# Layer 0's opening by pairs of feature tiles: norm, V and the first q and k from modulation quarters

## The chip, the core and the metric

One core of a Trainium2 chip runs the whole program once. The core has five engines with a queue each: TensorE (PE, matmuls into PSUM), VectorE (DVE), ScalarE (ACT), GpSimd (POOL) and SyncE (SP, which here issues nearly all DMAs). The metric is the device time of one execution in microseconds: 965.41 us as the median of 3 runs (965.35 to 966.09). Below, 1 MB is a million bytes, and a load of 1024 KB is 1.05 MB.

## The reference, cut to what matters

The network has 256 tokens of 1024 features, two transformer layers (attention, then a gated feed-forward) and a third layer with a convolution module. All of it is in 32-bit floats. Each norm is modulated by vectors that come from a conditioning vector c. What the change touches is the start of layer 0:

```python
c_act = jax.nn.silu(c)
mod = (c_act @ ada_w[0] + ada_b[0])[:, None, :]          # ada_w[0]: 1024 x 6144
sh_a, sc_a, g_a, sh_f, sc_f, g_f = jnp.split(mod, 6, axis=-1)
h = rms_norm(x, norm_g[0, 0]) * (1.0 + sc_a) + sh_a
q, k, v = jnp.split(h @ w_qkv, 3, axis=-1)               # w_qkv: 1024 x 3072, 8 heads of 128
```

Before the first projection can start, two of the six vectors (the scale sc_a and the shift sh_a) are needed; each is the product of c_act with a 1024 x 1024 block of ada_w[0], 4.19 MB. After that comes attention over 256 tokens with a bias by relative position, the output projection, and the feed-forward with the other four vectors.

## The kernel before, in words

Layout. The normed input is kept turned: `T` holds 8 feature tiles of 128 features (partitions) by 256 tokens. Every matmul operand is kept as a high part (a rounded 32-bit form for TensorE) and a low part (the rest), and `mm3` (L137 to L140) makes each product by three matmuls: high by high, high by low, low by high. A weight load (`load`, SP, L81) brings 1.05 MB into a raw buffer; `split` (L97 to L113) makes the high parts on ScalarE (L109, 1024 columns) and the low parts on VectorE (L111, 512 columns). `rows_unit` loads 256 rows by 1024 columns in runs of 4 KB, `cols_unit` and `half_unit` load 256-column blocks in runs of 1 KB. There are 4 raw buffers, and the first three loads rest in tiles that are not used yet (`spare`). The split parts have 8 buffers for high and 8 for low parts.

The opening. `first_norm` (L296) reads the two vectors' weights one after the other, each in four loads of 1.05 MB (the last in halves), and multiplies them with silu(c) on TensorE (`quads`, L232): the weights are the moving operand, the broadcast column of c the stationary one, four 32-column groups side by side. x is read behind the third load. The summed row gets its bias (L318), for the scale also one added and the gain multiplied (L320), is turned to columns by TensorE (L323, L325), and the normed and turned x (`nb`, L331 to L341) is multiplied by the scale columns on VectorE (L344). `shifted` adds the shift on ScalarE (L352) and makes the low part on VectorE (L353), two feature tiles at a time, ahead of each unit of the V projection.

Then `project` makes V in four units of 256 rows (`rows_matmul`, 512-column matmuls); units are loaded, split and multiplied one after the other. The bias tiles of attention are turned into `nb` by eight matmuls (L387). Pairs of heads follow: for each of four pairs, q and then k by `cols_matmul` (48 matmuls of 256 columns each), and the attention blocks of a pair run among the matmuls of the next pair (`step`). The output projection and the residual close the stage.

Background. The other 16 modulation vectors of the network are made by `mod_sum` (L204 to L218): four loads of 1.05 MB each, two products of 1024 columns per load on VectorE (L214, L216), ordered behind the newest split. `bg_step` is called after each unit and each q or k block, and `bg_plan` gives each stage a number of steps and of slots: in the first stage, 12 steps over 10 slots, the first two calls skipped. Those twelve steps are the three vectors that the end of this stage needs (the gate, the next scale, the next shift). A finished row is stored to DRAM (L226) and read back broadcast (`bcast_coef`, L181).

Order. Each engine works its queue in order. The order is not the text's: the framework's planner puts an instruction ahead of earlier ones that are not ready by its own reckoning (the copies of L448, traced in the first feed-forward, run at 2.5 us).

## Time and profile before

| what | value |
|---|---|
| median of 3 runs | 965.41 us |
| profiled execution, its own time | 965.92 us |
| its span, first to last instruction | 964.1 us |
| mean granted TensorE clock | 0.992 |
| HBM read, mean rate over the span | 240.94 MB, 252 GB/s |

The profiled execution is 0.5 us above the median, and 1.8 us of it lie outside the span. Times in rows are microseconds from the span's start. In a row `out<-in` names the tile written and the tiles read; `th` and `tl` are the high and low part of `T`, `h` and `l` (in the first unit `park`) those of a weight, `raw` a loaded weight. `[2.20 <-ACT park L109]` is the idle time of the engine before the instruction and what ended it. `x4` counts instructions.

### The profile page before, as it was taken

The page shows a single profiled execution, that of the slowest core. Times are in us where ns is not written, and L with a number is a line of the kernel's source. Part 1 is how long each engine was busy: PE and PEld are TensorE (multiplying, and loading weights), DVE is VectorE, ACT ScalarE, POOL GpSimd, SP SyncE. Part 2 cuts the span into 40 slices and gives each one's busy share as a digit, 9 for nine tenths or more (in the row PEclk, how much of TensorE's full clock was granted, in tenths as well). Part 3 has the DMA queues.
Part 4 walks back from the last instruction along what each step waited for, and adds up shares of the span by engine and source line. Part 5 has one row for each costly group of instructions (what it writes and reads, how often), then busy time and mean ns, then how long its engine had stood idle before and what let it go on. Part 6 is the DMA issues. An engine that isn't in the chain of part 4 may idle for free.

```text
span 964.1 us, 17220 instructions
## 1 busy us (share of the span) xinstructions
PE 929.8 (96%) x6687; PEld 812.9 (84%) x6687; DVE 765.9 (79%) x1461; ACT 495.1 (51%) x870; POOL 50.0 (5%) x118
## 2 busy tenths in 40 slices
PE   5899999999999999999999999999998999999997
PEld 2579977998999879876789999988897779999996
DVE  2778978977878798787999878888877789977774
ACT  2345666543344455685643444546416745655552
POOL 2100000000000010122100000001000100000000
PEclk9899999999999999999999999999999999999999
DMA  9988985978879859664589899886846366965511
GB/s 349 401 300 287 335 284 176 323 279 332 271 263 375 305 194 366 228 220 132 175 295 336 284 335 328 290 306 200 285 114 206 128 214 226 303 231 184 175 45 44
DMA packets 141519, 244.06 MB, mean 253 GB/s; under 512 B 6662, under 2 KB 106174, under 8 KB 141438
## 3 DMA queue, kind: packets, MB, share of 16 engines
q1 hardware_dynamic: 140918, 241.64, 72.2%
q0 software_dynamic: 496, 1.31, 0.4%
q8 instruction: 52, 0.85, 0.4%
q14 instruction: 29, 0.24, 0.1%
q10 hardware_dynamic: 24, 0.01, 0.0%
HBM read 240.94 MB, written 2.01 MB: 252 GB/s over the span
## 4 chain that ended last, share of the span: by engine, by line
issue 43%; PE 38%; DVE 7%; DMA 6%; ACT 3%; POOL 3%; SPq 1%; DVEq 0%; POOLq 0%; ACTq 0%
PE up L140 6%; PE up L139 6%; PE up L138 6%; PE acc L138 5%; PE acc L140 5%; PE acc L139 5%; DVE l L111 2%; DMA raw<-in_moba_w_qkv_dram 2%; DMA raw<-in_ada_w_dram 1%; DMA x<-in_x_dram 1%; PE acc L869 1%; ACT junk L485 1%; DMA raw<-in_ffn_w_in_dram 1%; POOL rstd L492 1%; PE up L659 1%
## 5 line engine op out<-in xcount | busy, mean ns | idle before, releaser
L111 DVE TENSOR_TENSOR l<-raw,h 128x512 fp32r<-128x512 f32 x548 | 354.6, 684 | 72.5 <-ACT h L109 70.2
L109 ACT ACTIVATE h<-raw 128x1024 fp32r<-128x1024 f32 x274 | 280.2, 1054 | 163.1 <-PE up L139 40.4
L140 PE MATMUL up<-th,l 128*128 128x256 f32 x640 | 181.6, 284 | 0.0
L139 PE MATMUL up<-tl,h 128*128 128x256 f32 x640 | 181.2, 283 | 0.0
L138 PE MATMUL up<-th,h 128*128 128x256 f32 x640 | 180.8, 283 | 0.0
L216 DVE SCALAR_TENSOR_TENSOR gemv<-raw,c_s,gemv 128x1024 f32<-128x1024 f32 x112 | 143.2, 1278 | 1.2 <-DMA raw<-in_ada_w_dram 0.2
L138 PEld LDWEIGHTS up<-th,h 128*128 128x128 f32 x640 | 121.0, 189 | 2.0 <-DVE m L759 0.4
L140 PEld LDWEIGHTS up<-th,l 128*128 128x128 f32 x640 | 120.7, 189 | 0.1
L139 PEld LDWEIGHTS up<-tl,h 128*128 128x128 f32 x640 | 120.4, 188 | 0.4
L138 PE MATMUL acc<-h,mh 128*128 128x512 f32 x232 | 91.6, 395 | 0.0
L139 PE MATMUL acc<-l,mh 128*128 128x512 f32 x232 | 90.7, 391 | 0.0
L140 PE MATMUL acc<-h,ml 128*128 128x512 f32 x232 | 90.4, 392 | 0.0
L140 PE MATMUL up<-oh,l 128*128 128x256 f32 x288 | 81.9, 284 | 0.0
L139 PE MATMUL up<-ol,h 128*128 128x256 f32 x288 | 81.8, 284 | 0.0
L138 PE MATMUL up<-oh,h 128*128 128x256 f32 x288 | 81.1, 282 | 0.0
L138 PE MATMUL acc<-th,h 128*128 128x256 f32 x256 | 74.9, 293 | 0.4 <-ACT h L109 0.4
L140 PE MATMUL acc<-th,l 128*128 128x256 f32 x256 | 73.3, 286 | 0.2 <-DVE l L111 0.2
L139 PE MATMUL acc<-tl,h 128*128 128x256 f32 x256 | 73.1, 286 | 0.0
L138 PEld LDWEIGHTS up<-oh,h 128*128 128x128 f32 x288 | 54.6, 190 | 0.8
L139 PEld LDWEIGHTS up<-ol,h 128*128 128x128 f32 x288 | 54.2, 188 | 0.7
L140 PEld LDWEIGHTS up<-oh,l 128*128 128x128 f32 x288 | 54.4, 189 | 0.1
L138 PEld LDWEIGHTS acc<-h,mh 128*128 128x128 f32 x232 | 43.6, 188 | 11.0 <-issue 1.6
(230 smaller groups left out, 1667.9 us busy)
## 6 DMA issues: line engine op xcount, KB each, us to landing
raw<-in_ada_w_dram SPq DMA_DIRECT2D x46, 1024.0 KB
raw<-in_ffn_w_in_dram SPq DMA_DIRECT2D x36, 1024.0 KB
raw<-in_mod_w_dram SPq DMA_DIRECT2D x24, 1024.0 KB
raw<-in_ffn_w_out_dram SPq DMA_DIRECT2D x22, 1024.0 KB
raw<-in_f_up_w_dram SPq DMA_DIRECT2D x18, 1024.0 KB
raw<-in_moba_w_qkv_dram SPq DMA_DIRECT2D x12, 1024.0 KB
raw<-in_diff_w_qkv_dram SPq DMA_DIRECT2D x12, 1024.0 KB
raw<-in_f_down_w_dram SPq DMA_DIRECT2D x11, 1024.0 KB
```

What stands on the lines that cost most here:

```text
L109: newest["high"] = nc.scalar.activation(h, r, AF.Copy).ins
L111: newest["split"] = nc.vector.tensor_sub(l[:, k], r[:, k], h[:, k].bitcast(F32)).ins
L138: nc.tensor.matmul(ps, lh, rh, start=start, stop=False, skip_group_check=True)
L139: nc.tensor.matmul(ps, lh, rl, start=False, stop=False, skip_group_check=True)
L140: last = nc.tensor.matmul(ps, ll, rh, start=False, stop=stop, skip_group_check=True).ins
L216: nc.vector.scalar_tensor_tensor(t, src, c[:, k:k + 1], t, op0=ALU.mult, op1=ALU.add)
L485: nc.scalar.activation(junk, src, AF.Square, scale=1.0 / 32, accum_out=ss[:, i:i + 1])
L492: nc.gpsimd.tensor_tensor(r, v, mhalf, op=ALU.pow)
L659: nc.tensor.matmul(po[:, 0:P], *(lr[::-1] if diff else lr), start=i == 0, stop=i == blk)
L869: mm = nc.tensor.matmul(ps[32 * g:32 * g + 32, 0:P], lw[t][:, m, g, :], ur[:, g, 4 * m:4 * m + P], start=m == 0, stop=m == 7, tile_positio ...
```

## The change

The two vectors are no longer read one after the other. `first_load` reads both at once in quarters of 256 columns, as eight DMAs of 0.26 MB (128 partitions, two runs of 1 KB each); the quarters rest in tiles of other uses (quarters 0 and 2 in the three coefficient tiles and the tile of the background sum, quarters 1 and 3 in the two q tiles and one buffer each of the split's high and low parts). `first_rows` reads and norms x first. `first_tiles` makes the scale and shift columns of two feature tiles from a quarter: quarters 0 and 1 by TensorE (8 matmuls of 512 columns, copied by ScalarE), quarters 2 and 3 by VectorE (8 products of 512 columns), then four one-column matmuls per quarter; two small VectorE operations apply bias, one and gain. ScalarE writes the high part straight from `nb` with scale and bias, and once more as a plain float, from which VectorE takes the low part.

`first_project` goes through four pairs of feature tiles: for each tile the V matmuls (four accumulators) and those of q and k of the first pair of heads (two accumulators). So pair 0 is finished with V, and the loop over pairs begins at pair 1. The q and k weights of pair 0 come by `half_unit` (512 rows by 256 columns of each). The bias tiles' loads are traced after the first quarter, their turning into `nb` after V. The silu of the second conditioning vector is ordered behind the norm. The first stage's background plan skips no call; with six calls in the pairs instead of eight and none in V, its twelve steps fall 2, 2, 1, 1, 1, 1 in pairs 1 to 3 and four in the output projection.

```diff
+FIRST_ON_PE = 2
...
-    def split(raw, blocks=False, rooms=None):
+    def split(raw, blocks=False, rooms=None, after=None):
...
-            newest["high"] = nc.scalar.activation(h, r, AF.Copy).ins
+            with tc.issue_after(after) if after else nullcontext():
+                newest["high"] = nc.scalar.activation(h, r, AF.Copy).ins
...
+    def rows_load(w, k0, c0):
+        return load(lambda raw: [(raw.rearrange("p (k n) -> p k n", k=2),
+                                  w[k0 * P:k0 * P + 256, c0:c0 + 1024].rearrange("(k p) n -> p k n", p=P))])
     def rows_unit(w, k0, c0, rooms=None):
-        return split(load(lambda raw: [(
-            raw.rearrange("p (k n) -> p k n", k=2),
-            w[k0 * P:k0 * P + 256, c0:c0 + 1024].rearrange("(k p) n -> p k n", p=P))]), rooms=rooms)
+        return split(rows_load(w, k0, c0), rooms=rooms)
...
+    pick = one.tile([P, 1], F32, name="pick")
+    nc.gpsimd.memset(pick, 0.0)
+    for i in range(4):
+        nc.gpsimd.memset(pick[32 * i:32 * i + 1, :], 1.0)
...
-        nc.scalar.activation(cs, c, AF.Silu)
-        return cs
+        return cs, lambda: nc.scalar.activation(cs, c, AF.Silu)
...
-    def mod_load(w, j, r, halved=False):
+    def mod_load(w, j, r):
...
-    def quads(ps, c, k, src, start, stop):
...
-    def first_norm(T):
...
+    def first_columns():
+        rows = work.tile([24, P], F32, name="rowsm", tag="w")
+        w, b, c = jobs[0][0], jobs[0][1], jobs[0][5]
+        for i, v in enumerate((b[D:2 * D], b[0:D], jobs[0][3])):
+            nc.scalar.dma_start(rows[8 * i:8 * i + 8, :], v.rearrange("(k p) -> k p", p=P))
+        ps = tr.tile([P, 512], F32, name="tr")
+        nc.tensor.transpose(ps[:, 0:24], rows, ident[:24, :24])
+        col = one.tile([P, 3, 8], F32, name="mcol")
+        nc.vector.tensor_copy(col.rearrange("p i k -> p (i k)"), ps[:, 0:24])
+        nc.vector.tensor_scalar(col[:, 0, :], col[:, 0, :], 1.0, None, op0=ALU.add)
+        return col
+    def first_rows():
+        for h in range(2):
+            nc.sync.dma_start(x[:, h, :], a["x"][0, h * P:h * P + P, :])
+        for h in range(2):
+            ss = small.tile([P, 2], F32, name="ss")
+            src = halves(x[:, h, :])
+            for n in range(2):
+                squares(ss, n, src[n])
+            r = rstd_of(ss)
+            for n in range(2):
+                t = two.tile([P, 512], F32, name="hn")
+                nc.vector.tensor_scalar(t, src[n], r, None, op0=ALU.mult)
+                ps = tr.tile([P, 512], F32, name="tr")
+                for q in range(4):
+                    nc.tensor.transpose(ps[:, q * P:q * P + P], t[:, q * P:q * P + P], ident)
+                ins = nc.scalar.activation(nb[:, 4 * n:4 * n + 4, h * P:h * P + P],
+                                           ps.rearrange("p (k n) -> p k n", k=4), AF.Copy).ins
+        return ins
+    def first_load(t):
+        w = jobs[0][0]
+        tiles = []
+        for i in range(4):
+            where, tag = (((coef, "coef"), (coef, "coef"), (coef, "coef"), (one, "gemv")),
+                          ((two, "q"), (two, "q"), (hlp, "h"), (hlp, "l")))[t % 2][i]
+            m = where.tile([P, 2, 2, 256], F32, name="fmod", tag=tag)
+            for n, j in enumerate((1, 0)):
+                nc.sync.dma_start(m[:, n], w[:, j * D + 256 * t:j * D + 256 * t + 256].rearrange(
+                    "(p r) n -> p r n", r=8)[:, 2 * i:2 * i + 2, :])
+            tiles.append(m)
+        return tiles
+    def first_tiles(T, t, rows, col, on_pe):
+        c = jobs[0][5]
+        g = two.tile([P, 2, 256], F32, name="fgem", tag="hn")
+        if on_pe:
+            ps = tr.tile([P, 512], F32, name="tr")
+            for r in range(8):
+                q = 32 * (r % 4)
+                nc.tensor.matmul(ps[q:q + 32, :], c[:, r:r + 1].to_broadcast([P, 32]), rows[r // 2][:, :, r % 2, :],
+                                 start=r < 4, stop=r >= 4, tile_position=(0, q), skip_group_check=True)
+            nc.scalar.activation(g.rearrange("p j n -> p (j n)"), ps, AF.Copy)
+        else:
+            for r in range(8):
+                src = rows[r // 2][:, :, r % 2, :]
+                if r == 0:
+                    nc.vector.tensor_scalar(g, src, c[:, 0:1], None, op0=ALU.mult)
+                else:
+                    nc.vector.scalar_tensor_tensor(g, src, c[:, r:r + 1], g, op0=ALU.mult, op1=ALU.add)
+        ps = tr.tile([P, 512], F32, name="tr")
+        for j in range(2):
+            for b in range(2):
+                nc.tensor.matmul(ps[:, 2 * j + b:2 * j + b + 1], g[:, j, b * P:b * P + P],
+                                 pick if on_pe else ones32[:, 0:1], start=True, stop=True, skip_group_check=True)
+        m = small.tile([P, 4], F32, name="fcols")
+        k = 2 * t
+        nc.vector.tensor_tensor(m, ps[:, 0:4], col[:, 0:2, k:k + 2], op=ALU.add)
+        nc.vector.tensor_tensor(m[:, 0:2], m[:, 0:2], col[:, 2, k:k + 2], op=ALU.mult)
+        for b in range(2):
+            v = work.tile([P, S], F32, name="fv", tag="w")
+            for d in (T[0][:, k + b, :], v):
+                nc.scalar.activation(d, nb[:, k + b, :], AF.Identity, scale=m[:, b:b + 1], bias=m[:, 2 + b:3 + b])
+            nc.vector.tensor_sub(T[1][:, k + b, :], v, T[0][:, k + b, :].bitcast(F32))
+    def first_project(w):
+        T = new_T("t")
+        col = first_columns()
+        turned = first_rows()
+        vals = [[acc.tile([P, 512], F32, name="acc") for _ in range(2)] for _ in range(2)]
+        qk = [up.tile([P, 512], F32, name="up") for _ in range(2)]
+        vw, qw = {}, {}
+        def load_v(u):
+            vw[u] = rows_unit(w, 2 * u, 2 * D)
+        def load_qk(u):
+            qw[u] = half_unit(w, u, (0, D))
+        def values(k):
+            wh, wl = vw[k // 2][k % 2]
+            for h in range(2):
+                for n in range(2):
+                    sl = slice(512 * n, 512 * n + 512)
+                    mm3(vals[h][n], *tok(T, k, h), wh[:, sl], wl[:, sl], k == 0, k == NK - 1)
+        def heads(k):
+            wh, wl = (t[:, k % 2, :] for t in qw[k // 4][k // 2 % 2])
+            for i in range(2):
+                for b in range(2):
+                    sl = slice(256 * i + 128 * b, 256 * i + 128 * b + 128)
+                    mm3(qk[i][:, 256 * b:256 * b + 256], wh[:, sl], wl[:, sl], T[0][:, k, :], T[1][:, k, :],
+                        k == 0 and b == 0, k == NK - 1)
+        def tiles_of(t):
+            first_tiles(T, t, mods.pop(t), col, t < FIRST_ON_PE)
+        mods = {0: first_load(0)}
+        raw = {0: rows_load(w, 0, 2 * D)}
+        mods[1] = first_load(1)
+        tiles_of(0)
+        next(bias)
+        with tc.issue_after(turned):
+            make_c2()
+        vw[0] = split(raw.pop(0), after=turned)
+        load_qk(0)
+        for t in range(NK // 2):
+            if t < 3:
+                load_v(t + 1)
+            if t + 2 < 4:
+                mods[t + 2] = first_load(t + 2)
+            if t == 1:
+                load_qk(1)
+            if t + 1 < 4:
+                tiles_of(t + 1)
+            for k in (2 * t, 2 * t + 1):
+                values(k)
+                heads(k)
+        return T, qk, vals
...
-        for h, ps in project(T, w_qkv, 2 * D, ("oh", "ol"), before=first):
-            for n in range(2):
-                nc.scalar.activation(v[:, h, 512 * n:512 * n + 512], ps[n], AF.Copy)
+        pairs = []
+        scale = -float(DH // (2 if diff else 1)) ** -0.5
+        def pair(pq, pk):
+            q = two.tile([P, 2, S], F32, name="q")
+            nc.scalar.activation(q, pq.rearrange("p (b n) -> p b n", b=2), AF.Copy, scale=scale)
+            yield
+            kk = two.tile([P, 2, S], F32, name="kk")
+            nc.scalar.activation(kk, pk.rearrange("p (b n) -> p b n", b=2), AF.Copy)
+            pairs.append((q, kk))
         if first:
+            T, qk, vals = first_project(w_qkv)
+            for h, ps in enumerate(vals):
+                for n in range(2):
+                    nc.scalar.activation(v[:, h, 512 * n:512 * n + 512], ps[n], AF.Copy)
+            for _ in pair(*qk):
+                pass
             next(bias)
             lam_col()
+        else:
+            for h, ps in project(T, w_qkv, 2 * D, ("oh", "ol")):
+                for n in range(2):
+                    nc.scalar.activation(v[:, h, 512 * n:512 * n + 512], ps[n], AF.Copy)
...
-        for i in range(4):
+        if first:
+            heads(0)
+        for i in range(len(pairs), 4):
...
-    plans = ((12, 10, 2), (16, 17), (12, 12), (20, 17), (0, 0), (4, 4, 4))
+    plans = ((12, 10, 0), (16, 17), (12, 12), (20, 17), (0, 0), (4, 4, 4))
```

## Rows read from the trace of the kernel before

**Rows 1.** Page part 1: busy us, share of span, instructions, by engine.

```profile
PE 929.8 (96%) x6687; PEld 812.9 (84%) x6687; DVE 765.9 (79%) x1461; ACT 495.1 (51%) x870; POOL 50.0 (5%) x118
```

**Rows 2.** Waits of PE in 0 to 32 us: total, times, longest.

```profile
PE acc L232 <- DMA raw<-in_ada_w_dram: 10.8, 6, 7.0
```

**Rows 3.** Chain of waits, 0 to 60 us: start, us, what.

```profile
2.67 11.27 DMA x<-in_x_dram
...
22.32 6.55 DMA raw<-in_ada_w_dram
```

**Rows 4.** Timeline of PE: start, us, engine, line, operation, count, idle before.

```profile
23.25 1.93 PE L232 MATMUL acc<-raw,c_s 128*32 128x256 f32 x32
...
32.75 0.80 PE L138 MATMUL acc<-park,th 128*128 128x512 f32 x1 [2.20 <-ACT park L109]
...
60.15 1.88 PE L387 MATMUL tr<-toep,stage 128*128 128x512 f32 x4
...
74.04 0.28 PE L140 MATMUL acc<-th,l 128*128 128x256 f32 x1
74.16 0.28 PE L138 MATMUL acc<-th,h 128*128 128x256 f32 x1
```

**Rows 5.** Windows: length, busy PE, PEld, DVE, ACT, POOL; clock, DMA share, GB/s.

```profile
0.00:10.00 10.00, 1.94 (x16) 0.69 (x16) 1.43 (x5) 1.70 (x3) 3.81 (x14) 1.00 0.78 266
10.00:20.00 10.00, 6.55 (x49) 2.99 (x50) 1.86 (x4) 4.08 (x10) 1.97 (x4) 0.87 1.03 405
20.00:30.00 10.00, 7.26 (x84) 3.19 (x83) 4.14 (x14) 1.08 (x2) 1.28 (x2) 0.96 1.03 409
```

**Rows 6.** Windows of pair 0's k and pair 1's q.

```profile
66.00:72.00 6.00, 5.39 (x43) 4.99 (x42) 4.12 (x6) 2.49 (x3) 0.00 (x0) 1.00 1.06 379
72.00:78.00 6.00, 6.00 (x53) 6.00 (x52) 5.13 (x9) 2.85 (x4) 0.00 (x0) 1.00 1.05 375
```

**Rows 7.** Page part 5: ScalarE's split, the high part.

```profile
L109 ACT ACTIVATE h<-raw 128x1024 fp32r<-128x1024 f32 x274 | 280.2, 1054 | 163.1 <-PE up L139 40.4
```

**Rows 8.** Windows of the V projection.

```profile
32.70:38.00 5.30, 5.25 (x13) 4.15 (x14) 5.27 (x10) 4.44 (x7) 0.00 (x0) 0.52 1.03 384
38.00:57.50 19.50, 19.50 (x85) 15.55 (x83) 16.48 (x21) 6.62 (x9) 0.00 (x0) 1.00 0.99 377
```

**Rows 9.** Groups of 32 to 80 us: ScalarE's feature rows of layer 0.

```profile
L352 ACT ACTIVATE th<-nb,col 128x256 fp32r<-128x256 f32 x6 | 2.7, 494 | 0.0
```

**Rows 10.** Groups of VectorE, 73.4 to 137.9 us.

```profile
L111 DVE TENSOR_TENSOR l<-raw,h 128x512 fp32r<-128x512 f32 x43 | 28.1, 685 | 2.6 <-ACT h L109 2.5
L216 DVE SCALAR_TENSOR_TENSOR gemv<-raw,c_s,gemv 128x1024 f32<-128x1024 f32 x11 | 14.1, 1278 | 0.0
```

**Rows 11.** Windows of pairs 1 to 3 and the output projection.

```profile
73.40:118.00 44.60, 44.60 (x366) 42.85 (x364) 41.01 (x96) 27.05 (x62) 0.00 (x0) 1.00 0.90 321
118.00:138.00 20.00, 19.39 (x109) 15.32 (x108) 14.87 (x44) 13.72 (x34) 0.00 (x0) 1.00 0.87 276
...
100.00:120.00 20.00, 20.00 (x164) 18.69 (x163) 18.54 (x47) 14.94 (x35) 0.00 (x0) 1.00 0.91 334
```

**Rows 12.** Timeline of SP's queue, 104 to 140 us.

```profile
104.64 10.06 SPq L81 DMA_DIRECT2D raw<-in_moba_w_o_dram  x4
120.29 0.53 SPq L226 DMA_DIRECT2D scratch<-row  x1
120.86 1.39 SPq L181 DMA_DIRECT2D coef<-scratch  x3
122.35 17.93 SPq L81 DMA_DIRECT2D raw<-in_ffn_w_in_dram  x9
```

**Rows 13.** Timeline: VectorE's last output-projection split, TensorE's first feed-forward matmul.

```profile
126.31 1.88 DVE L111 TENSOR_TENSOR l<-raw,h 128x512 fp32r<-128x512 f32 x3
...
148.26 0.39 PE L138 MATMUL up<-park,th 128*128 128x512 f32 x1
```

**Rows 14.** Waits of SP's queue in 0 to 45 us: total, times, longest.

```profile
SPq L81 <- DMA raw<-in_ada_w_dram: 12.7, 5, 3.8
```

89 lines of the change are left out of this document (10 added, 79 removed).

## The prediction

> **What bounds the kernel now.** I read the page's busy times first. TensorE is busy in 96% of the span [rows 1], so a change pays only where TensorE now waits, and it loses wherever it adds TensorE work or a new wait. Next come the waits of TensorE in the first 32 us: 10.8 us go to DMAs of the modulation weights [rows 2]. The chain of waits says what stands there: x lands at 2.67 + 11.27 = 13.94 us, and the last modulation piece ends 6.55 us after 22.32 us [rows 3]. The timeline then shows the first V matmul at 32.75 us, released by ScalarE's split of the first V weights, and the last matmul of pair 0 (q and k) at 74.04; pair 1 starts at 74.16 [rows 4]. The windows show DMA at its rate throughout: 405 and 409 GB/s between 10 and 30 us [rows 5]. So the opening is bound by bytes: two modulation vectors of 4.19 MB each must be in before any projection can start, and after 32.75 us TensorE is bound by its own work. The reader is to see that the opening is the only large hole.
>
> The quantity I work out is the start of pair 1, 74.16 us now. All TensorE work after it is the same in both kernels, so the time moves with it, less what is given back later.
>
> **Bytes up to pair 1.** The new order on SP is x (1.05 MB), modulation quarter 0 (2.10), V rows 0 (1.05), quarter 1, q/k half 0, V rows 1, quarter 2, V rows 2, quarter 3, q/k half 1, V rows 3: 15.7 MB, and 1.05 MB of bias tiles beside them. x and V (5.24 MB) come in 4 KB runs, at 0.405 MB/us [rows 5]: 12.9 us. Quarters, q/k and bias tiles (11.5 MB) come in 1 KB runs. Their rate follows from the stretch where 1 KB column loads and 4 KB modulation loads alternate at 379 and 375 GB/s [rows 6]: 2/0.377 - 1/0.405 gives 0.353 MB/us, so 32.7 us. The first 10 us moved 2.66 MB [rows 5], as if a full-rate stream began at 3.4 us. x landed 1.4 us after its bytes (3.4 + 3.67/0.405 = 12.5, against 13.94 [rows 3]). The last V rows thus land at 3.4 + 12.9 + 32.7 + 1.4 = 50.4 us. One ScalarE split, 1.05 us [rows 7], and the last two feature tiles follow: 24 V matmuls at 19.5/85 = 0.23 us [rows 8] and 24 of 256 columns at 0.12 us [rows 4], 8.4 us. By bytes pair 1 starts at 59.9 us.
>
> A rule bears on this. The modulation loads become 32 DMAs of 0.26 MB in place of DMAs of 0.5 and 1 MB. The Trainium skill (DMA: Bandwidth & Descriptors, section Bandwidth) asks for transfers of 1 MiB or more, and its fit in the section on the anatomy of a DMA (2.0 us plus bytes over 436 GB/s, for the GpSimd path) gives, as an estimate from that page, 2.6 us for each, 83 us for the 32 if they ran one by one. The windows of 10 to 30 us [rows 5] show a queue kept at its rate by several DMAs in flight, which is against reading the rule that way here; no row shows DMAs of this size in a stream.
>
> **TensorE up to pair 1.** x, quarter 0 and V rows 0 land at 3.4 + 5.2 + 5.9 + 1.4 = 15.9 us. ScalarE then makes four feature rows at 0.49 us [rows 9] and one split: the first V matmul comes at 19.0, 13.7 us earlier than now. From there: 96 V matmuls, 22.2 us; 96 of 256 columns, 11.4; the start at half clock, where 13 matmuls took 5.30 us at a granted 0.52, nearly all of it at the 1.2 GHz level, after an engine that had stood 2.2 us [rows 4, 8], in place of 3.0 us, so 2.3; two modulation quarters on TensorE, 16 instructions of 512 columns each, against 32 of 256 in 1.93 us [rows 4], so 1.9 us each; the column picks, four small ones per quarter, bounded by nothing and by 1 us, taken at 0.9, so 3.6; the bias flips, 2 us (four take 1.88 while other matmuls run among them [rows 4]). Sum 19.0 + 22.2 + 11.4 + 2.3 + 3.8 + 3.6 + 2.0 = 64.3 us, if TensorE never waits. If flips and picks fall into waits for data, the bytes decide: 60. If the clock stays at the lower level for the first two quarters, half of the projection work takes twice as long, up to 16.8 us more. I take 64, as the work row is the longer: a gain of 10 us in the start of pair 1.
>
> What is removed costs nothing more: the row path (transposes, row and gain adds, eight scalings, x behind the modulation) stood before 32.75 and goes whole. What is added on other engines hides in a stage paced by bytes: eight more feature rows on ScalarE, 4 us over 45; on VectorE 16 half-length products for quarters 2 and 3, some 0.64 us each by half of 1.28 [rows 10], 10.2 us. From 27 to 52 us VectorE then has those, three units of V and one of q/k (four subtractions each, at 28.1/43 = 0.65 us [rows 10]) and the low parts, about 22 us in 25: covered, but only just. The ACT queue's three small loads change shape, not number; the silu of the second c moves behind the norm and is needed only in layer 2; the bias-tile loads on POOL's queue are in the byte sum.
>
> **What is late next: VectorE in pairs 1 to 3 and the output projection.** The background plan changes from 12 steps over ten slots that all lie before the output projection to 8 in the blocks of pairs 1 to 3 and 4 in that projection. Each step is 1.05 MB and two products of 1.28 us. Between 73.4 and 138 us VectorE is busy 41.0 + 14.9 = 55.9 of 64.6 us, with 11 of these long products and one short one, 14.8 us [rows 10, 11]. All 24 would be 30.7, so 15.9 us come in. Two steps (5.1 us) can be done between the last V rows and pair 1, and six subtractions for the next stage (3.9 us) can slide: 62.8 of 64.6 us. TensorE now stays full with VectorE at 18.54 of 20 us [rows 11], 93%; at that share 60 us fit, so 3 us come out as TensorE waits for split weights. Bounds: nothing, if VectorE's 8.7 us of idle time there close up, and 10.8 us, the 15.9 less the two early steps, if none does. I take 3, by the stretch at 93%.
>
> The last vector of that plan also comes later. Now its store is issued at 120.29, its broadcast loads follow at 120.86, and the feed-forward loads stand behind them in SP's queue at 122.35 [rows 12]; they are first used at 148.26 [rows 13]. Afterwards the twelfth step stands behind the last output-projection split, which ends at 128.2 now [rows 13]; four steps of 2.56 us put it at 138.4 on the old clock. If the feed-forward loads stay behind it (some 2.5 us for store and broadcast, then the 9.9 us that the first one takes now, 122.35 to 132.2, and a split), 5 us show. If SP is given them earlier, as the four output-projection loads at 104.64 stand ahead of the store, nothing shows. I take nothing, by that row.
>
> **Sum.** 10 - 3 = 7 us. The profiled execution took 965.92 us (span 964.1, 1.8 around it), so 958.9; the median of the three runs is 0.5 lower, so 958.4 for the median, written 958.5.
>
> **Rivals.**
> First, nothing is given back: flips and picks fall into waits, pair 1 starts near 61, VectorE's waits close up: 965.4 - 13 = 952. For it: VectorE's idle time in that stretch is mostly waiting. Against: the stage is full on three engines. Chance 0.20.
> Second, VectorE and the hand-over take nearly all: 9 us or 4 + 5 instead of 3, so 964, between 962 and 967. For it: the 62.8 of 64.6 us. Against: SP's order at 104.64. Chance 0.18.
> Third, the stages do not interleave as written, because quarter 3 rests in buffers that splits and the first pair's q also use, and what follows in SP's queue (q/k half 1, V rows 3) waits with it. SP waits for such releases today: 12.7 us behind landed DMAs alone in the first 45 us [rows 14]. If quarter 3 starts 6 us late, pair 1 starts at about 68 to 70 and VectorE gives back 1: 962. Chance 0.12.
> Fourth, slower: the 32 small DMAs do not keep the rate. The 8.39 MB of quarters take 23.8 us at 0.353; below about 0.24 MB/us they take 11 us more, the 7 us gain and the 4 us by which TensorE's sum exceeds the byte sum are gone, and from there the kernel loses. At half the rate it is 24 us more: 965.4 - 7 - 4 + 24 = 978. The rule on transfer size in the Trainium skill (DMA: Bandwidth & Descriptors, section Bandwidth) speaks for this rival. Against it: SP issues three loads in 1.39 us, 0.46 each [rows 12], and the bytes of one small DMA take 0.74 us, so the queue can be kept filled. Chance 0.08.
>
> **How the numbers follow.** The forecast has 0.42, with a range of its own from 955 to 962. A measurement of this kernel tells 0.2%, 1.9 us, from no change. Faster than 963.5: 0.42 + 0.20 + 0.10 + 0.06 = 0.78. Within: 0.10 from the second and third. Slower than 967.3: 0.08 of the fourth and 0.04 of the second, 0.12. The range of 949.5 to 967 leaves out 0.08 above with the fourth, some of the second, and a little below.
>
> **What would show it.** Right: the first V matmul near 19 us; DMA at 350 GB/s or more up to 50; the last V rows landing near 50; pair 1's first matmul at 60 to 66; VectorE over 90% busy from there to the end of the output projection, with new TensorE waits on its subtractions of some 3 us in all. The forecast is wrong if pair 1 starts after 70, if the granted clock stays at 0.5 beyond the first quarter, if the quarters move below 250 GB/s, or if TensorE stands over 5 us at the start of the first feed-forward.

## The result, and the profile after

The changed kernel takes 973.06 us (median of 4 runs, 971.29 to 973.66) against 965.75 us (965.35 to 967.46) beside it: a ratio of 1.0069, interval 1.0054 to 1.0085. It is slower by 0.7%; 958.5 was forecast, and the range ended at 967. Its profiled execution is the quickest of the four: 971.29 us, span 969.5, so the profile holds 5.4 us of span to be found, of 7.3 between the medians; what the slower executions add is not seen in it.

Two instants cut the loss: the start of pair 1 (74.16 before [rows 4]) and the transposes of the second token half's feed-forward norm. TensorE's timeline has them (start, us, engine, line, operation, count, idle before), first of the kernel before, then of the changed one:

```profile
156.52 0.60 PE L527 MATMUL tr<-ident,hn 128*128 128x128 f32 x4
```

```profile
68.95 3.69 PE L465 MATMUL tr<-toep,stage 128*128 128x512 f32 x8
72.08 0.68 PE L142 MATMUL acc<-th,h 128*128 128x256 f32 x1
...
162.55 0.60 PE L605 MATMUL tr<-ident,hn 128*128 128x128 f32 x4
```

The bias flips end at 72.64, and pair 1 is in full course at 72.6: 1.5 us earlier than before, where 10 were forecast. From there to the second half's norm it takes 89.9 us, before 82.4: 7.5 given back, where 3 were forecast. Behind that norm 0.6 us come back (its distance to the end of the span is 807.6 us before, 807.0 after). -1.5 + 7.5 - 0.6 = 5.4.

**The opening.** Windows of the changed kernel, columns as in [rows 5]:

```profile
10.00:20.00 10.00, 6.31 (x40) 4.33 (x38) 2.02 (x7) 5.24 (x11) 1.28 (x3) 0.98 1.08 358
20.00:30.00 10.00, 8.43 (x35) 3.36 (x35) 2.16 (x7) 4.66 (x7) 0.53 (x1) 0.67 1.08 365
30.00:40.00 10.00, 10.00 (x47) 8.50 (x48) 9.86 (x18) 5.44 (x8) 2.10 (x3) 0.84 1.06 364
40.00:50.00 10.00, 8.34 (x53) 7.42 (x52) 8.21 (x15) 1.11 (x3) 0.00 (x0) 1.00 1.08 362
50.00:60.00 10.00, 10.00 (x52) 8.57 (x51) 9.56 (x20) 8.47 (x12) 0.00 (x0) 0.83 0.92 316
```

The DMAs of 0.26 MB, among the larger ones of V, q and k, keep 358 to 365 GB/s up to 50 us, as the byte sum had it; with 4 KB runs it was 405 and 409 GB/s [rows 5], so a tenth is lost and not half. The Trainium skill (DMA: Bandwidth & Descriptors, section Bandwidth) asks for 1 MiB or more per transfer; the trace does not bear that out as a limit on each DMA of a stream. The granted clock does not keep up: 0.67, 0.84, and again 0.83 after 50 us. The timelines of TensorE, ScalarE and VectorE show why:

```profile
20.83 1.65 PE L142 MATMUL acc<-h,th 128*128 128x512 f32 x3 [3.56 <-ACT h L111]
22.41 1.44 PE L449 MATMUL tr<-stage 32*8 32x384 f32 x2
23.79 3.21 PE L352 MATMUL tr<-fmod,c_s 128*32 128x512 f32 x16
...
27.72 1.05 PE L365 MATMUL tr<-pick,fgem 128*128 128x1 f32 x8 [0.30 <-ACT fgem L354]
...
29.84 0.80 PE L143 MATMUL acc<-l,th 128*128 128x512 f32 x1 [0.43 <-DVE l L113]
...
49.54 0.50 PE L142 MATMUL acc<-h,th 128*128 128x512 f32 x1 [1.66 <-ACT th L374]
```

```profile
17.76 0.60 ACT L374 ACTIVATE th<-nb,fcols 128x256 fp32r<-128x256 f32 x1 [1.66 <-DVE fcols L370]
...
19.74 1.99 ACT L111 ACTIVATE h<-raw 128x1024 fp32r<-128x1024 f32 x2
```

```profile
23.89 0.55 DVE L450 TENSOR_SCALAR stage<-tr 8x384 f32<-8x384 f32 x1 [3.60 <-PE tr L449]
...
28.81 0.16 DVE L369 TENSOR_TENSOR fcols<-tr,mcol 128x4 f32<-128x4 f32 x1 [4.13 <-PE tr L365]
29.01 0.16 DVE L370 TENSOR_TENSOR fcols<-fcols,mcol 128x2 f32<-128x2 f32 x1
29.09 5.50 DVE L113 TENSOR_TENSOR l<-raw,h 128x512 fp32r<-128x512 f32 x9
```

The first V matmul comes at 20.83 (19.0 forecast): ScalarE's first feature row starts at 17.76, behind quarter 0's copy, picks and two column operations, for which the forecast had no time on this path. The three high-by-high products run, and then TensorE does other things until 29.84: the bias row, quarter 1's products and picks. The low parts of the first V rows, whose high parts are done at 21.73, stand in VectorE's queue behind the bias row (L450) and quarter 1's columns (L369, L370), which wait for TensorE. VectorE is idle for 7.7 us there, 6.3 of them with the low parts ready to be made, and then has 9.86 us of work in 10.

**The hand-over.** TensorE's wait before the norm's transposes, in the changed kernel, then VectorE's queue ahead of it, SP's queue, and one window:

```profile
PE tr L605 <- DVE hn L600: 4.5, 1, 4.5
```

```profile
144.41 2.50 DVE L113 TENSOR_TENSOR park<-raw,park 128x512 fp32r<-128x512 f32 x4
146.83 4.30 DVE L113 TENSOR_TENSOR l<-raw,h 128x512 fp32r<-128x512 f32 x7
151.05 1.41 DVE L600 SCALAR_TENSOR_TENSOR hn<-hn,rstd,coef 128x512 f32<-128x512 f32 x2
```

```profile
130.50 7.14 SPq L82 DMA_DIRECT2D raw<-in_ffn_w_in_dram  x5
142.18 0.53 SPq L232 DMA_DIRECT2D scratch<-row  x1
142.75 1.02 SPq L82 DMA_DIRECT2D raw<-in_ffn_w_in_dram  x2
143.98 0.34 SPq L189 DMA_DIRECT2D coef<-scratch  x1
```

```profile
150.00:156.00 6.00, 3.94 (x14) 2.70 (x15) 6.00 (x11) 4.16 (x7) 0.34 (x1) 0.73 1.09 356
```

The last row is stored at 142.18, before at 120.29 [rows 12]; SP did put five feed-forward loads ahead of it, but five more stand behind it (SP waits 4.5 us for the row with the store at its head), the norm's shift waits, and eleven low parts go ahead of the norm. TensorE stands 4.47 us and then runs at a granted 0.73. So I began with two theories: **A**, single instructions at the wrong place of in-order queues hold up the opening, and **B**, the late last row is what the stretch behind it pays for. The rivals to both: VectorE's amount of work.

### The profile page after: what moved, and what is told of

Its sections match the earlier page's. It is cut to its first block, busy times and chain, and to the rows that moved or that the text cites. A ratio compares the mean times of both kernels' runs of the same rounds, so it can differ in the third digit from the quotient of the medians.

```text
span 969.5 us, 17156 instructions
## 1 busy us (share of the span) xinstructions
PE 930.6 (96%) x6620; PEld 814.4 (84%) x6620; DVE 772.4 (80%) x1474; ACT 501.5 (52%) x880; POOL 53.2 (5%) x122
## 3 DMA queue, kind: packets, MB, share of 16 engines
q1 hardware_dynamic: 147446, 241.64, 72.9%
## 4 chain that ended last, share of the span: by engine, by line
issue 42%; PE 39%; DVE 7%; DMA 4%; ACT 4%; POOL 3%; SPq 0%; DVEq 0%; POOLq 0%; ACTq 0%
PE acc L143 6%; PE acc L142 6%; PE acc L144 6%; PE up L144 5%; PE up L143 5%; PE up L142 5%; DVE l L113 2%; DVE z L947 2%; ACT h L111 1%; ACT junk L563 1%; POOL rstd L570 1%; POOL var L568 1%; PE up L735 1%; DMA ud<-up 1%; DMA raw<-in_moba_w_o_dram 1%
## 5 line engine op out<-in xcount | busy, mean ns | idle before, releaser
L144 PE MATMUL up<-th,l 128*128 128x256 f32 x672 | 190.3, 284 | 0.0
L143 PE MATMUL up<-tl,h 128*128 128x256 f32 x672 | 190.2, 283 | 0.0
L142 PE MATMUL up<-th,h 128*128 128x256 f32 x672 | 190.0, 283 | 0.0
L142 PEld LDWEIGHTS up<-th,h 128*128 128x128 f32 x672 | 127.1, 189 | 2.4 <-DVE ml L857 0.4
L143 PEld LDWEIGHTS up<-tl,h 128*128 128x128 f32 x672 | 126.4, 188 | 0.7
L144 PEld LDWEIGHTS up<-th,l 128*128 128x128 f32 x672 | 126.6, 189 | 0.2
L142 PE MATMUL acc<-th,h 128*128 128x256 f32 x224 | 65.7, 293 | 0.0
L143 PE MATMUL acc<-tl,h 128*128 128x256 f32 x224 | 63.9, 285 | 0.0
L144 PE MATMUL acc<-th,l 128*128 128x256 f32 x224 | 63.4, 283 | 0.0
```

Source lines behind the costliest of these rows:

```text
L142: nc.tensor.matmul(ps, lh, rh, start=start, stop=False, skip_group_check=True)
L143: nc.tensor.matmul(ps, lh, rl, start=False, stop=False, skip_group_check=True)
L144: last = nc.tensor.matmul(ps, ll, rh, start=False, stop=stop, skip_group_check=True).ins
```

## The experiments

Each was timed in rounds with the kernel before on the same chip; e4, e8, e12 and e15 are told below. Flips is the end of the bias flips (72.6 in the changed kernel), norm the start of the second half's norm transposes (162.55), stretch the difference, all in us from the profiled run. Runs are compared with each other by their ratios.

| run | time | ratio, interval | flips | norm | stretch |
|---|---|---|---|---|---|
| e1 twelve steps in six calls | 974.99 | 1.0090, 1.0073-1.0107 | 73.5 | 166.5 | 93.0 |
| e2 low parts first | 970.48 | 1.0040, 1.0026-1.0053 | 70.0 | 159.6 | 89.6 |
| e3 quarters all on TensorE | 973.14 | 1.0076, 1.0057-1.0095 | 75.0 | 165.8 | 90.8 |
| e5 order as written | 971.57 | 1.0054, 1.0038-1.0069 | 70.8 | 162.7 | 91.9 |
| e6 nothing waits for the last row | 972.54 | 1.0065, 1.0052-1.0078 | 72.9 | 163.7 | 90.8 |
| e7 order, two steps early | 975.00 | 1.0090, 1.0071-1.0110 | 70.0 | 165.6 | 95.6 |
| e9 order, all on TensorE | 969.67 | 1.0042, 1.0027-1.0057 | 71.1 | 160.2 | 89.1 |
| e10 last vector on TensorE | 973.72 | 1.0093, 1.0075-1.0110 | 72.1 | 164.7 | 92.7 |
| e11 e9 and e10 | 974.33 | 1.0089, 1.0076-1.0103 | 71.5 | 166.0 | 94.6 |
| e13 e6 without its loads | 971.10 | 1.0055, 1.0042-1.0068 | 72.7 | 160.4 | 87.7 |
| e14 four steps early | 971.18 | 1.0060, 1.0048-1.0073 | 78.2 | 162.2 | 84.0 |
| e16 no last vector | 965.31 | 0.9991, 0.9982-1.0000 | 73.4 | 156.1 | 82.7 |
| e17 all steps in the pairs | 975.76 | 1.0102, 1.0088-1.0116 | 70.4 | 165.3 | 94.9 |
| e18 e14, row held | 970.64 | 1.0050, 1.0035-1.0064 | 71.2 | 160.8 | 89.6 |

### The opening: e2, e3, e5, e9

**e2** holds quarter 1's columns behind the low parts of the first V rows:

```diff
-            nc.vector.tensor_tensor(m, ps[:, 0:4], col[:, 0:2, k:k + 2], op=ALU.add)
+        with tc.issue_after(after) if after else nullcontext():   # after: the first V rows' split, for t = 1
+            nc.vector.tensor_tensor(m, ps[:, 0:4], col[:, 0:2, k:k + 2], op=ALU.add)
```

> Only an order differs from the changed kernel: VectorE's column operations of quarter 1 are held behind the four low-part subtractions of V rows 0. Theory A (in VectorE's queue those subtractions stand behind columns that wait for TensorE, so V's first products starve): the first subtraction comes before 23 us instead of 29.1, pair 1 starts at 66 to 69 instead of 72.1, the time is 967 to 970. Rival B (the opening is paced by its bytes, DMA being busy to 50 us): pair 1 starts within 1 us of 72. Rival C (VectorE's amount of work from 29 to 60 us paces it): also within 1.5 us of 72, since the amount is the same.

Flips end 2.6 us earlier and the kernel gains, less than expected: TensorE still had 3.51 us of quarter 1's products ahead of the low parts.

**e3** makes quarters 2 and 3 on TensorE too:

```diff
-FIRST_ON_PE = 2
+FIRST_ON_PE = 4
```

> All four quarters are multiplied by TensorE instead of two (the 16 half-length products leave VectorE). Theory A (order of the first quarters): pair 1 starts within 2 us of 72.1, the hand-over wait stays, time 971 to 975. Rival C (VectorE's amount of work paces the opening): pair 1 starts 4 us or more earlier, at 68 or less, and the time is 969 or less. Rival B (bytes): pair 1 within 1 us of 72.

VectorE is busy 3.49 and 5.11 us in the windows 40:50 and 50:60 (8.21 and 9.56 in the changed kernel), TensorE waits nowhere there, and the flips end 2.4 us later. This is no clean test of VectorE's amount of work: the edit gives TensorE two quarters more, about 3.8 us (1.92 each in e9), and the first stretch at the lower clock was longer too (a granted 0.50 from 20 to 28 us). What it shows is that the wait for the first low parts stays (0.4 us) with VectorE 9 us freer.

**e5** is e2 with TensorE's order mended too: quarter 1's products behind the first tile's V products, the bias row behind them.

```diff
-        tiles_of(0)
-        next(bias)
+        tiles_of(0)
...
+                if k == 0:
+                    tiles_of(1)     # its TensorE products ordered behind the newest V matmul
+                    next(bias)
```

> The changed kernel with its opening in the order in which the text of the prediction had it: quarter 1's TensorE products stand behind the V products of the first feature tile, the bias row's transposes behind those, and VectorE makes the low parts of the first V rows and of the first q/k half before quarter 1's columns. Theory A (the order of the queues in the opening holds TensorE back): no TensorE work of quarter 1 between the first three V matmuls and the low-part matmuls, first low-part matmul near 24 us, bias flips at 62 to 64 us (68.95 in the changed kernel, 66.35 with VectorE's columns alone held back), and with the hand-over's 5 us still there a time of 965 to 968 us. Rival (VectorE's amount of work, or the bytes, pace the opening): flips stay at 66 or later, 970 us or more.

The low-part matmuls start at 21.59, 8 us earlier, and the flips still end at 70.8: the loss moved to the next such place. VectorE's timeline of e5, then the one wait of TensorE between its first V matmul and 75 us:

```profile
44.51 0.16 DVE L372 TENSOR_TENSOR fcols<-tr,mcol 128x4 f32<-128x4 f32 x1 [1.58 <-PE tr L367]
44.59 2.50 DVE L113 TENSOR_TENSOR l<-raw,h 128x512 fp32r<-128x512 f32 x4
47.01 0.16 DVE L373 TENSOR_TENSOR fcols<-fcols,mcol 128x2 f32<-128x2 f32 x1
```

```profile
PE acc L142 <- ACT th L377: 2.2, 1, 2.2
```

Four subtractions, 2.50 us together, were put between the two small operations that make quarter 2's columns. TensorE stands 2.2 us, and its clock in 48 to 52 us is 0.64.

**e9** adds FIRST_ON_PE = 4 to e5 and traces each quarter behind the V products of the first tile of the pair before.

> The opening in the order of e5, with quarters 2 and 3 too on TensorE and each quarter's products traced behind the V products of the tile before. In e5 TensorE lost 3.0 us to waits after its first V matmul and 5.4 us to two stretches at half clock (20.9 to 28.7 and 47.9 to 50.8 us), the second after the 2.2 us that it waited for quarter 2's columns, which had an L113 group of four in front of them in VectorE's queue. Theory A (single instructions at the wrong place in in-order queues): no wait over 0.5 us between 25 and 65 us, no second half-clock stretch, flips done at 66 to 68 us (70.8 in e5, 72.6 in the changed kernel). Rival (data arrive too late anyhow): the quarter or V waits stay, flips done at 70 or later. The hand-over is untouched: time 967 to 970 us.

Between 25 us and the norm TensorE has only the wait for the last row (5.2 us), and up to that the clock stays at 1.00 from 30 us on. The flips end at 71.1. So this is what TensorE's own work takes from 20.8 us on in e9, and it holds two quarters, 3.8 us, that the forecast had on VectorE. Without them it would be 67.3, by this estimate; no run shows an order that reaches it, and 64 is 3 us below even that.

### The late row: e1, e4, e6, e8

**e1** puts all steps into the six calls of the pairs:

```diff
-    plans = ((12, 10, 0), ...
+    plans = ((12, 6, 0), ...
```

> Only the first stage's background plan differs from the changed kernel: 12 steps over 6 slots, so all twelve fall, two each, into the q and k blocks of pairs 1 to 3 and none into the output projection. Theory A (the last vector comes too late for the hand-over to the feed-forward): TensorE's 4.5 us wait for the normed rows at the hand-over falls below 1 us, its first feed-forward matmul comes near 148.5 us instead of 153.6, and the time is 967 to 969. Rival (VectorE has too much work in this stage wherever the steps stand): the wait moves into the pairs, pair 1 to the output projection takes 4 us more, and the time stays at 972 to 974.

The 4.47 us wait goes (0.5), and TensorE waits 1.7 us for the background sums and 2.4 for low parts instead: slower.

**e4** and **e8** give the kernel before the late last vector, e4 by its plan, e8 by a list of the steps in each call:

```diff
-    plans = ((12, 10, 2), ...      # steps per call 2, 2, 1, 1, 1, 1, 1, 1, 1, 1
+    plans = ((12, 12, 4), ...      # e4
+    [2, 2, 1, 1, 1, 1, 0, 0, 0, 0, 1, 1, 1, 1]      # e8
```

> The kernel before with only its first plan changed: the first four calls skipped, then one step in each of 12 calls, eight in the pairs and four in the output projection, as late as in the changed kernel. Theory A (hand-over): a TensorE wait of 4 to 6 us appears ahead of the first feed-forward, which starts near 153 instead of 148.3, and the time is 969 to 972; the opening up to 74 us is the same. Rival (the wait comes from the changed opening, not from the plan): time within 2 us of before.

> The kernel before with its opening, and four of its twelve background steps (the last vector) moved from pairs 2 and 3 into the output projection, one step per unit, as in the changed kernel. Theory B: a TensorE wait of 4 to 6 us before the feed-forward norm's transposes, first feed-forward matmul at 152.5 to 154.5 us (148.26 before), time 970 to 972 us. Rival (the hand-over costs only because the changed opening left VectorE behind): first feed-forward matmul within 1 us of 148.26, time 965 to 966.5 us.

e4 took 981.04 us (ratio 1.0165, 1.0141 to 1.0189), but it does not answer: the planner moved the bias flips into the opening, where TensorE waited 9.8 us for their DMA. e8 kept the opening, and took 966.16 us (ratio 0.9993, 0.9984 to 1.0002), with its norm at

```profile
156.72 0.60 PE L529 MATMUL tr<-ident,hn 128*128 128x128 f32 x4
```

0.2 us from before. Four steps in the output projection cost nothing by themselves.

**e6** lets nothing wait for the late row:

```diff
-        return bcast_coef(scratch[slot])
+        return bcast_coef(scratch[4 if slot == 3 else slot])
```

> The changed kernel in which the feed-forward's shift of layer 0 is read from the row of the scale, which is in DRAM a vector earlier; the shift's own row is still computed, with all its loads and products, but nothing waits for it (the shift in that norm is thereby left out of the computation). The opening is unchanged. Theory B (the hand-over: the twelfth step stands behind the output projection, its row, store and broadcast hold the norm, and the feed-forward's low parts stand ahead of that norm in VectorE's queue): the 4.47 us wait of TensorE before the norm's transposes goes, first feed-forward matmul at 148 to 149 us, time 967 to 969 us. Rival (VectorE's backlog would show anyway): the wait comes back on the low parts of the first feed-forward weights, first matmul or the next ones late by 3 us or more, time 972 or more.

The rival, almost to the number. The waits of TensorE in e6, 118 to 175 us:

```profile
PE up L143 <- DVE park L113: 1.9, 1, 1.9
PE up L142 <- ACT h L111: 1.6, 1, 1.6
PE tr L605 <- DVE hn L600: 0.4, 1, 0.4
```

The wait came back on the feed-forward's first weights. Theory B falls as far as the norm's wait goes. The row's store is still there: SP waits 6.8 us with it at its head, and five feed-forward loads stand behind it.

### What the four steps cost: e10, e13, e16, and e12

In the 24 products of the three vectors, the kernel before has 12 behind 73.4 us [rows 10]; the changed one has 20 behind its flips. Is it VectorE's work (**theory C**) or the loads, which hold raw buffers and stand in SP's queue (**theory D**)?

**e10** makes the last vector's products by TensorE, 8 matmuls and one addition per step:

```diff
+        if slot == 3:
+            row = one.tile([P, 256], F32, name="prow")
+            for r in range(4):
+                raw = mod_load(w, j, r)
+                ...   # 8 matmuls of 256 columns as in the old quads()
+                nc.vector.tensor_add(row, ps[:, 0:256], row if r else bq)
```

> The changed kernel, with the products of the last of the three background vectors made by TensorE (eight 256-column matmuls and one VectorE addition of 256 columns per step) in place of VectorE's eight products of 1.28 us. The loads, their order of tracing, the store and the broadcast stay; VectorE has some 9 us less to do after pair 1 and TensorE 2 us more. Theory C (the change moved four steps behind the start of pair 1, and VectorE's total there is the limit: pair 1 to the second half's norm takes 90 us against 82.4 before; the late row is only where it shows): that stretch falls to 85 to 87 us, the 4.5 us wait at the norm to under 1.5, time 967 to 970 us. Rival D (the four steps' loads, 4.2 MB and their raw buffers, are the limit): the stretch stays at 89 to 92 us, time 973 to 975.

The late-row wait is gone, the stretch is no shorter. TensorE's group of the new products in 72 to 165 us, and SP's timeline of e10:

```profile
L245 PE MATMUL tr<-raw,c_s 128*32 128x256 f32 x64 | 6.1, 387 | 0.0
```

```profile
129.29 0.38 SPq L82 DMA_DIRECT2D raw<-in_ffn_w_in_dram  x1
137.71 0.53 SPq L232 DMA_DIRECT2D scratch<-prow  x1
138.29 0.99 SPq L82 DMA_DIRECT2D raw<-in_ffn_w_in_dram  x2
```

The row's store stands in SP's queue for 8 us, with the feed-forward's loads behind it; TensorE then waits 2.4 us for their low parts. But the products also keep TensorE busy for 6.1 us, not 2: of the 92.7 us that much is the test's own price, and the waits fall from 5.1 us in the changed kernel to 3.4. So e10 does not refute theory C.

**e13** is e6 with the last vector's four loads gone and its products made from x:

```diff
-            raw = mod_load(w, j, r)
+            raw = mod_load(w, j, r) if c is not c1 or w is not jobs[0][0] or j != 3 else None
...
-                src = raw[:, 1024 * kk:1024 * kk + 1024]
+                src = x[:, kk, :] if raw is None else raw[:, 1024 * kk:1024 * kk + 1024]
```

> The changed kernel with the last vector's four loads left out: its eight products read the resident x in place of the weights, and the feed-forward's shift is read from the scale's row, as in e6 (both vectors are thereby wrong in the computation; VectorE's work, the stores and the broadcasts stay). Compared with e6, the four loads alone are gone. Theory D (loads and raw buffers: each background load holds one of four buffers until VectorE has done its products, and the feed-forward's first weights queue behind them on SP): the first feed-forward weights are issued at 122 to 126 us in place of 130.5, no TensorE wait over 1 us between 145 and 165, second half's norm at 155 to 159 us in place of 163.7 in e6, time 965 to 968 us. Theory C (VectorE's total): stays at 162 or later, 971 or more.

The first feed-forward loads are issued at 120.19, 10 us earlier than in the changed kernel; the stretch loses 3.1 us of e6's and stays 5.3 above the kernel before. TensorE still waits 2.9 us for low parts. The last of VectorE's products ends at 138.3, some 20 us ahead of the longest of these waits, so that the products cause them is not shown.

**e16** takes the vector away altogether.

```diff
+            if slot == 3:
+                done.add(slot)
+                continue
...
-    plans = ((12, 10, 0), ...
+    plans = ((8, 6, 0), ...
```

> The changed kernel without the last of its three background vectors: neither loads nor products nor store (the shift of layer 0's feed-forward norm is left out and the scale's row is read in its place); the other eight steps stand in pairs 1 to 3 as before the change, none in the output projection. Theory E (the four steps cost by two resources, each of which is enough by itself): pair 1 to the second half's norm back at 82 to 84 us, no TensorE wait over 1 us there, time 964 to 966.5 us, that is no gain of the opening beyond its 1.5 to 2 us. If 88 us or more remain, the four steps are not the cause, and the loss comes from the opening's backlog.

Norm row of e16:

```profile
156.07 0.60 PE L608 MATMUL tr<-ident,hn 128*128 128x128 f32 x4
```

The stretch is 82.7 us, 82.4 before, no wait over 0.3 us is left in it, and the kernel comes to 965.31 us. Products, loads and store of the four steps together are the loss of the stretch. How it divides between them is not shown: e10 has its own price on TensorE, and e13 keeps the row's store.

**e12** gives the kernel before the changed kernel's spread: no step in V.

```diff
-    plans = ((12, 10, 2), ...
+    [0, 0, 0, 0, 2, 2, 1, 1, 1, 1, 1, 1, 1, 1]
...
+                with tc.issue_after(newest["mm"]):
+                    nc.tensor.matmul(ps, flip, tp[:, 512 * j:512 * j + 512], start=True, stop=True)
```

> The kernel before with the changed kernel's spread of background steps: none in the V projection, 2, 2, 1, 1, 1, 1 in pairs 1 to 3 and four in the output projection (the bias flips are held behind the last V matmul, so that they stay where they were). Its opening is otherwise as it was. Theory C: pair 1 to the second half's norm grows from 82.4 to 87 to 91 us, time 970 to 974 us. Rival (the loss of the changed kernel comes from its opening: VectorE enters pair 1 with work left over, buffers hold quarters): no more than 1 us is lost, 965 to 967 us.

976.29 us (ratio 1.0112, 1.0097 to 1.0128). The planner changed the V projection as well, and this wait of TensorE in it is most of the loss, so the time does not answer:

```profile
PE acc L139 <- DVE park L111: 7.3, 1, 7.3
```

The stretch answers in part. Pair 0's k is copied as pair 1 starts, at 74.35 in the kernel before; in e12, with its norm:

```profile
80.35 0.60 ACT L726 ACTIVATE kk<-acc 128x512 f32<-128x512 f32 x1 [5.09 <-PE acc L140]
165.57 0.60 PE L531 MATMUL tr<-ident,hn 128*128 128x128 f32 x4
```

So pair 1 starts 6.0 us late, at some 80.2, and the stretch is 85.4, 3.0 above the kernel before, between theory C and its rival, with 17 of the 24 products behind that start. Set beside the others, the stretch grows with that count: 12 products, 82.4 (before) and 82.7 (e16); 15, 84.0 (e14, below); 17, 85.4 (e12); 20, 89.9 (changed). e18, with 17, falls out of the row at 89.6, for a reason given below. The openings differ, so these are cases and no law.

### Looking for a better kernel: e7, e11, e14, e15, e17, e18

**e7**: e5, with one call more.

```diff
                 load_v(t + 1)
+            else:
+                bg_step()
...
+    plans = ((12, 8, 0), ...
```

> The order of the opening as in the run beside it, and the twelve background steps two at the end of the opening, eight or nine in pairs 1 to 3, and the last one in the output projection's first unit. Theories A and B together: flips at 63 to 65 us, no wait over 1 us before the first feed-forward matmul, which comes at 139 to 143 us, time 957 to 961 us, faster than the kernel before. If VectorE's amount of work from pair 1 on is the bound (the rival that won with all steps in six calls, 974.99 us), TensorE waits of 4 us and more stand in the pairs and the time stays at 964 or more.

**e11**: the edits of e9 and e10 together.

> The opening of e9 and the last vector of e10 together. Theories A and C: the two gains add, flips done at 66 to 68 us, 84 to 87 us from pair 1 to the second half's norm, time 961 to 965 us: not slower than the kernel before, perhaps faster by up to 0.5%. If one limit stands behind both, the sum is less than either: 968 or more.

**e14**: e9, with steps traced with the second to fourth pair of feature tiles.

```diff
+            if t >= 1:
+                bg_step()
...
+    [1, 1, 2, 1, 1, 1, 1, 1, 1, 1, 1, 0, 0]
```

> The opening of e9, with one background step behind the second and third pair of feature tiles each and two behind the last, then one per call, eight of them, none in the last two units of the output projection: four steps are done before pair 1, as in the kernel before. Theories C and D both: pair 1 to the second half's norm back at 82 to 84 us; if pair 1 still starts near 71 us (e9) the time is 961 to 964 us, faster than the kernel before by 0.2 to 0.5%. Rival (the opening has no room: bytes or VectorE): pair 1 starts 3 us or more later, or TensorE waits in pair 1 for its weights, and the time is 966 us or more.

**e15**:

```diff
-    rawp = pool("rawp", 4)
+    rawp = pool("rawp", 5)
...
-    work = pool("work", 10)
+    work = pool("work", 7)
```

> The changed kernel with five raw buffers in place of four (the small work buffers go from ten to seven to make the room). Theory D: SP stalls less between 112 and 140 us, the first feed-forward weights are issued before 128 us (130.5), the stretch from pair 1 to the second half's norm shrinks by 2 to 5 us, time 968 to 971 us. Theory C, or if the smaller work pool costs as much: 972 us or more.

**e17**: e11 with e1's plan, `((12, 6, 0), ...`.

> The opening of e9, the last vector's products on TensorE, and all twelve steps in pairs 1 to 3 (two per call): VectorE has eight steps there, as many as in the kernel before after pair 1 starts, no load or store of a row stands among or behind the output projection's last loads. Theory E: pair 1 at 71 to 72 us, 84 to 86 us to the second half's norm (2 us of TensorE products more than before), time 963 to 966 us, the first order of the new opening that is not slower than the kernel before. If the twelve steps' loads hold up the pairs' own weights, TensorE waits in the pairs and the time is 968 or more.

**e18**: e14, with the row's summing matmuls traced one call later and held.

```diff
+            with tc.issue_after(newest["mm"]):
+                nc.tensor.matmul(ps[32 * q:32 * q + 32, 0:256], ones32, ...
```

> e14 with one difference: the first background row's four summing matmuls and what follows them are traced and ordered behind pair 1's q block, so that TensorE does not stand before them ahead of the bias flips (4.1 us in e14, and a half-clock stretch behind it). If the opening has room for four steps, flips done at 71 to 73 us, 82 to 84 us from pair 1 to the second half's norm, time 962 to 966 us: as fast as the kernel before or faster. If it has no room, the wait comes back on pair 1's first low parts, which VectorE makes behind six products of 1.28 us, by 3 us or more, and the time is 967 or more.

None beats the kernel before. e7, e11 and e17 lose more than e9: with two steps in a call TensorE waits in the pairs for background sums (e7: 3.0 us, e17: 1.1), at the feed-forward low parts are late again (1.9, 3.1 and 2.4 us), and e11 and e17 have e10's products on TensorE. e14 shows the short stretch, 84.0, but pays in the opening:

```profile
PE tr L244 <- DVE gemv L223: 4.1, 1, 4.1
```

In e18 that wait is gone, the flips end at 71.2, and the place is in pair 1. Windows of e18, then a row of VectorE's timeline:

```profile
72.00:78.00 6.00, 4.93 (x36) 4.33 (x37) 4.31 (x11) 3.75 (x7) 0.00 (x0) 1.00 0.99 321
78.00:84.00 6.00, 3.50 (x30) 2.55 (x29) 3.44 (x6) 2.77 (x4) 0.00 (x0) 1.00 0.44 150
84.00:90.00 6.00, 6.00 (x39) 6.00 (x40) 5.30 (x11) 1.83 (x4) 0.00 (x0) 0.72 0.97 329
```

```profile
80.56 0.42 DVE L248 TENSOR_TENSOR row<-tr,bquad 128x256 f32<-128x256 f32 x1 [4.21 <-PE tr L245]
```

TensorE is idle for 3.6 of the first 12 us, and the clock of the next six is 0.72. This is the opening's fault once more: the row's addition waits 4.21 us at the head of VectorE's queue for the summing matmuls that the edit held back, and the row's store 5.6 us at the head of SP's, with pair 1's low parts and loads behind them. So e18 does not show that four steps have no room in front of pair 1; I found no place for them, and a place with the row out of the way was not tried. e15 took 978.46 us (ratio 1.0135, 1.0119 to 1.0150) with the stretch at 90.0 and the further loss in later stages; that the smaller work pool causes it is not shown, and the run does not decide on the buffers.

## Why the prediction was wrong

**"Sum 19.0 + 22.2 + 11.4 + 2.3 + 3.8 + 3.6 + 2.0 = 64.3 us, if TensorE never waits ... I take 64": the step that failed first.** Measured 72.6. The first V matmul was 1.8 us late, by the hand-over from quarter 0 to the feature rows. Half clock cost more than 2.3 us; windows of the changed kernel:

```profile
20.00:24.00 4.00, 3.17 (x9) 1.14 (x13) 0.40 (x2) 1.73 (x2) 0.00 (x0) 0.50 1.10 353
24.00:28.00 4.00, 3.70 (x20) 0.86 (x12) 0.61 (x2) 0.93 (x2) 0.53 (x1) 0.70 1.04 383
28.00:32.00 4.00, 3.57 (x16) 2.97 (x17) 3.15 (x7) 4.00 (x7) 1.58 (x3) 0.73 1.10 350
32.00:36.00 4.00, 4.00 (x20) 3.37 (x20) 4.00 (x8) 1.42 (x2) 0.52 (x1) 0.84 1.06 395
...
48.00:52.00 4.00, 2.46 (x7) 1.99 (x8) 3.96 (x9) 3.11 (x6) 0.00 (x0) 0.79 1.05 376
52.00:56.00 4.00, 4.00 (x21) 3.39 (x20) 3.61 (x7) 2.76 (x3) 0.00 (x0) 0.78 0.92 339
```

A granted c in 4 us means 8(1 - c) us at the lower level: 3.2 of the first (TensorE starts there at 20.83), 2.4, 2.2, 1.3, then 1.7 and 1.8. Work there takes twice its time: 4.5 and 1.7 us lost, 3.9 more than in the sum. Waits (0.3, 0.43 and 1.66) add 2.4. The flips took 3.69 us, not 2: there are eight, and the row that I priced them by [rows 4] has four. The bias row was not in the sum, 0.8 at full clock (e9; half of its 1.44 here is in the clock's term). Against that, the sum put quarter 0's matmuls and picks, 2.8 us, behind the first V matmul, where they stand ahead of it. 1.8 + 3.9 + 2.4 + 1.7 + 0.8 - 2.8 = 7.8 of 8.3; the rest is open. The condition "if TensorE never waits" was priced for clock and data, not for the order in which VectorE's queue gets its instructions. e9 has the waits and the second clock stretch away and still ends at 71.1, with 3.8 us of products that the sum had on VectorE.

**"covered, but only just" (VectorE from 27 to 52 us)** counted work against time and was right as a count (VectorE is busy 21.2 of these 25 us). It left out that VectorE stands idle for 7.7 us in front of it, waiting at the head of its queue.

**"so 3 us come out" and "I take nothing, by that row": the step that turned the sign.** The two were separate items, 3 and 0; together they are 7.5 us (pair 1 to norm), 4.5 of it the wait and some 1.6 the half clock behind it (3.2 us at the lower level in 150:156); the pairs themselves took 0.5 longer (pair 1 to 118.2, before to 119.2). The whole stretch, changed and before:

```profile
72.64:162.55 89.91, 84.55 (x555) 72.72 (x553) 81.87 (x175) 54.62 (x119) 7.43 (x8) 0.98 0.79 278
```

```profile
74.16:156.52 82.36, 81.40 (x547) 71.85 (x546) 71.68 (x165) 54.55 (x120) 3.88 (x8) 1.00 0.83 283
```

VectorE has 10.2 us more to do, and only 2.6 of that came out of its idle time (10.7 before, 8.0 now). It is busy 91% of the stretch, close to the 93% of the sum, and the two early steps came as the sum had them (10.2 us more against its 15.9 - 5.1 = 10.8). The term that does not fit the trace is "six subtractions for the next stage (3.9 us) can slide": low parts for that stage are what the norm then stands behind, eleven of them, 6.6 us from 144.41 on. That it would come earlier without them was not tried. SP put half of the loads ahead of the row and half behind. In e6 the stretch is as long with hardly a wait of the norm; e16 shows that the four steps themselves cost it. The rival "VectorE and the hand-over take nearly all: 9 us" was nearest in size for this and had a wrong opening under it.

**Right:** what bounds the opening before (with the bytes reordered, the first V matmul came 12 us earlier); the rate of the small DMAs, against the fourth rival; first V matmul within 2 us; VectorE over 90% busy behind the opening; that the last row would come behind the output projection's splits. The third rival's start of pair 1, 68 to 70, was nearest. SP did wait 5.6 us for TensorE to free quarter 3's buffers, as it said, but TensorE waited for nothing that came behind them; the time went in VectorE's and TensorE's queues.

**Open:** how much of the stretch is VectorE, how much the loads and how much the row's store at the head of SP's queue (e10 and e13 also changed the planner's order, and e10 TensorE's work); why this plan of steps costs 3.0 us behind the old opening (e12, 17 products behind the start of pair 1) and 7.5 behind the new one (20); and whether four steps fit into the new opening.

## What to carry to other kernels

Where a stage is rebuilt so that three engines hand small results to each other, write down the order of each in-order queue before summing work: a 0.16 us instruction at its head that waits for another engine costs everything behind it, and TensorE pays again at half clock. Work that used to hide in the old, slower stage (here four background steps in the V projection) must be given a new place in the sum, with its loads and its products counted as two claims on two queues. Before a test moves work off one engine, price it on the other: 64 short matmuls cost e10 6.1 us where 2 were expected. The stage that was slow was also where the slack was.

## What the runs showed of the hardware

TensorE's granted clock fell after short stands in the middle of a full stage: after 1.66 us of idle time (with eight one-column matmuls ahead of it) 3.4 us at the lower level followed, so 1.7 us were lost on top; after 2.2 us in e5 a granted 0.64 in 48 to 52 us, 1.4 lost; after 4.47 us at the hand-over 1.6 lost. In e9, which has one-column matmuls too but does not stand there, it is 1.00. Not every stand did it: in e10 TensorE waits 1.9 us before 162.2, and the granted clock is 1.00 up to 170.
